# First head of a gated attention layer: four columns side by side from unnormalised x, the norm from x with tokens on partitions, and four plain gate columns

## The chip, the core and the metric

The kernel runs on one core of one Trainium2 chip. The metric is the device time of one execution in microseconds (us). The core's engines have queues of their own: TensorE (PE, with its weight loads PEld), VectorE (DVE), ScalarE (ACT), GpSimd (POOL) and SyncE (SP), which here issues nearly all transfers. They wait for each other by semaphores.

## What is computed

One layer with 512 tokens and a model width of 2048, all in float32, cut to what matters here:

```python
hn = rmsnorm(x, norm_g)                       # x: 512 tokens x 2048
proj = hn @ w_in                              # 3 branches x (q, k, v, gate) x 4 heads x 128 columns,
                                              # 4 forget logits, 3 x 2048 merge gate logits
...
yc = stick_breaking_attention(q, k, v)        # branch C, the first whose heads are computed here
ys = stack(ya, yb, yc) * silu(gate)
up = einsum('bsnw,nwd->bsnd', ys, w_up)
merged = sum(sigmoid(gates + b_gate) * up)
return x + merged @ w_out
```

`rmsnorm` divides each token by the root of the mean square over its 2048 values and multiplies by a gain for each of the 2048. A product of x with a weight column can therefore be made with the gain alone, and be multiplied by the token's factor afterwards.

## The kernel before

All activations lie transposed: 128 model values on the partitions, 512 tokens along the free side, sixteen such tiles of x (`xraw`, from `xT`). To keep float32's accuracy every operand is split into a high part (a copy on ACT, rounded to the product's format) and a low part (a subtraction on DVE), `split_to`, lines 91 to 93; a product of two operands is then three (`mm3`, lines 100 to 103).

The work of PE is a list of `units`. A unit has one weight tile of 8 k tiles x 128 columns (512 KB), loaded on SP, split on ACT and DVE (`prep`, two units ahead, `LA = 2`), and 24 products. There are two forms. A **plain column** (`col_task`) takes two units, one for each half of the 2048 rows, with 24 products of 512 tokens each. A **pair** (`pair_task`) computes two columns by Strassen's form in Winograd's variant: seven units with 24 products of 256 tokens each, in place of the four units of two plain columns. For that form the weight quarters are added on DVE (lines 315 to 327), the seven results are added up on DVE, and x is needed in other shapes: with x1 = [B11 | B12] and x2 = [B21 | B22] (halves of the model width by halves of the tokens) the parts B11, B21, B22, T1 = B12 - B11, T2 = B22 - T1, T3 = B22 - B12 and T4 = T2 - B21.

The first head (branch C, head 0) is made of plain columns, since it starts before the norm is known: `prep_x` (lines 217 to 230) splits x times its gain into `xs` and squares x on ACT; DVE and POOL add the squares up. Its ten units are: half of the forget logits (`f_units`, 16 products of 8 columns), q and k's first halves, the other half of the logits, q and k's second halves, then v and the gate. `norm_x` (line 244) sums the squares over the partitions by a product with ones, takes the root (`rsqrt`), and leaves the token factors `rstd`; it stands behind unit 1 with high priority. The column results are multiplied by `rstd` as they leave PSUM (`scaled`, line 626). From unit 3 on `combos(k)` multiplies x by gain and norm (line 255, DVE), forms T1 to T4's sums on POOL (lines 257 to 260) and splits them; `parts1` and `parts2` behind units 7 and 9 split the normalised x1 and x2, over the unnormalised ones. Two pairs of gate columns follow, and all further heads (q and k's pair, a gate pair, v and gate's pair, a gate pair). The stages of each head's attention are hung onto later units by `at(unit, work)`.

Tile's scheduler orders each engine's instructions by a simulation, except where a `manual_schedule` region keeps some engines in the order written: before, PE up to unit 17 (`OFF["man"]`, line 853). Pools: 21 tiles of 128x512 (`t2`), 56 for split x (`xt`), six raw weight tiles, three of each split weight, four PSUM tiles `acc` and four `att`.

Of the kernel before, what the change touches and what calls it, by code (L numbers as in the profile page):

```python
# [15 lines left out]
P = 128  # L16
S = 512
# [8 lines left out]
UK = 8  # L26
HS = S // 2
# [11 lines left out]
def hybrid_kernel(  # L39
    ctx: ExitStack,  # L40
    tc: tile.TileContext,
    xT: bass.AP,
    consts: bass.AP,
# [61 lines left out]
    # ------------------------------------------------------------------ constants  # L105
# [18 lines left out]
    class Unit:  # L124
        """A stretch of the tensor engine's work with one stationary operand of up to 8 k tiles."""
# [8 lines left out]
    def load(u):  # L134
        u.raw = []
        for s, keep in u.srcs:
            t = raw_tile(u.shape)
            nc.sync.dma_start(t, s)
            u.raw.append(t)
            if keep is not None:  # L140
                keep.append(t)
# [10 lines left out]

    for kt in range(4):
        load_x(kt)
# [18 lines left out]
    # -1 where key k >= j: suffix sums inside a block  # L173
# [4 lines left out]
    # A, rows are queries: NEG where the key (free) is after the query  # L178
# [4 lines left out]
    # C, rows are keys: valid where the query (free) is after the key  # L183
# [7 lines left out]
    # column h has ones on the rows h, 32 + h, 64 + h, 96 + h  # L191
# [6 lines left out]
    # the query gains carry the softmax scale  # L198
# [9 lines left out]
    t4 = [xt("t4") for _ in range(UK)]  # L208
    x1 = [(xt("x1h"), xt("x1l")) for _ in range(UK)]
    t23 = [(xt("t23h"), xt("t23l")) for _ in range(UK)]  # L210
    x2 = [(xt("x2h"), xt("x2l")) for _ in range(UK)]
    xs = x1 + x2
    ssq = [None, None]
    first_ps = att()
    sqp = [att(), att()]

    def prep_x(kt):
        x = xraw[kt]
        h, lo = xs[kt]
        if kt % 2:  # L220
            nc.vector.tensor_scalar_mul(h, x, gn[:, kt:kt + 1])
        else:
            nc.scalar.activation(h, x, AF.Copy, scale=gn[:, kt:kt + 1])
        nc.vector.scalar_tensor_tensor(lo, x, gn[:, kt:kt + 1], f(h), op0=ALU.mult, op1=ALU.subtract)
        s = sqp[kt // 2 % 2] if kt % 2 and kt > 1 else t2("sq")
        nc.scalar.activation(s, x, AF.Square)
        if kt < 2:
            ssq[kt] = s
        else:
            (nc.gpsimd, nc.vector)[kt % 2].tensor_add(ssq[kt % 2], ssq[kt % 2], s)  # L230

    def rsqrt(y, ps, n):
        """y = (ps / n + EPS) ** -0.5: a guess by exp and ln, and one Newton step."""
        t, w, v = t2("rt"), t2("rw"), t2("rv")
# [4 lines left out]
        nc.vector.tensor_mul(w, w, v)  # L239
        nc.vector.scalar_tensor_tensor(y, w, 1.5, t, op0=ALU.add, op1=ALU.mult)  # L240

    rstd = []

    def norm_x():
        ps = att()
        for i in range(2):
            nc.tensor.matmul(ps, onef, ssq[i], start=i == 0, stop=i == 1)
        rstd.append(t2("rstd"))
        rsqrt(rstd[0], ps, D)

    def combos(k):
        """The rows of x at their norm, and what Strassen's form needs of them beside the parts."""
        a, b = xraw[k], xraw[k + UK]
        for x, kt in ((a, k), (b, k + UK)):
            nc.vector.scalar_tensor_tensor(x, x, gn[:, kt:kt + 1], rstd[0], op0=ALU.mult, op1=ALU.mult)  # L255
        t, u = t2("t23"), t2("t4")
        nc.gpsimd.tensor_sub(t[:, RH], b[:, RH], a[:, RH])
        nc.gpsimd.tensor_sub(a[:, RH], a[:, RH], a[:, LH])
        nc.gpsimd.tensor_sub(t[:, LH], b[:, RH], a[:, RH])
        nc.gpsimd.tensor_sub(u[:, LH], t[:, LH], b[:, LH])  # L260
# [10 lines left out]
    # ------------------------------------------------------------------ projections  # L271
# [12 lines left out]
    def col_task(srcs, xs, evac):  # L284
        """A column tile as it stands; two units, one for each half of the rows."""
# [92 lines left out]
    # ------------------------------------------------------------------ attention  # L378
# [9 lines left out]
    def f_units():  # L388
        """The four heads' logits: the columns' high and low parts side by side."""
        w2 = cp.tile([P, KT, 2 * NH], F32R, name="w2")  # L390
        nc.vector.tensor_copy(w2[:, :, :NH], wf)
        nc.vector.tensor_sub(w2[:, :, NH:], wf, f(w2[:, :, :NH]))
        ps = first_ps

        def mms(i):
            def go(u):
                for kt in range(i * UK, (i + 1) * UK):
                    for j in range(2):
                        nc.tensor.matmul(ps[:2 * NH, :], w2[:, kt, :], xs[kt][j],
                                         start=kt + j == 0, stop=kt + j == KT)  # L400
            return go
        return [Unit(None, None, mms(i)) for i in range(2)], ps
# [4 lines left out]
    def forget_bias():  # L407
        """log sigmoid of the logits, their running sums, and the two sides of c[q] - c[k]."""
# [8 lines left out]
        # log1p(u) = 2 atanh(u / (2 + u))  # L417
# [29 lines left out]
    def tri(name, dt=F32):  # L447
        """Four tiles of 512, 384, 256 and 128 columns in three slots."""
        t = [t2(name, dt) for _ in range(3)]
        return [t[0], t[1][:, :S - P], t[2][:, :S - 2 * P], t[1][:, S - P:]]  # L450

    def head_stages(n, h, st):
        """The stages of a head's attention, as (units after the end of q and k, work)."""
# [110 lines left out]
        def av():  # L564
# [8 lines left out]
            # sigmoid(g) = exp(min(g, 0) - log(1 + exp(-|g|)))  # L573
# [26 lines left out]
    # ------------------------------------------------------------------ the order of the work  # L600
# [22 lines left out]
    def scaled(st, r):  # L623
        def evac(ps):
            st[r] = t2("c")
            nc.vector.tensor_mul(st[r], ps, rstd[0])
        return evac

    def first_head(n, h):
        st = {}  # L630
        fu, fps = f_units()
        c = {r: col_task(col(n, r, h), xs, scaled(st, r)) for r in (Q, K, V, G)}
        units.extend([fu[0], c[Q][0], c[K][0], fu[1], c[Q][1], c[K][1],
                      c[V][0], c[G][0], c[V][1], c[G][1]])

        def norm_first():
            with tc.high_priority():
                norm_x()
        at(1, norm_first)
        for k in range(UK):  # L640
            at(OFF["c0"] + k // OFF["c1"], lambda k=k: combos(k))

        def parts1():
            for k in range(UK):
                split_to(*x1[k], xraw[k])

        def parts2():
            for k in range(UK):
                split_to(*x2[k], xraw[k + UK])
            v = t2("f")[:2 * NH, :]  # L650
            nc.vector.tensor_mul(v, fps[:2 * NH, :], rstd[0][:2 * NH, :])
            nc.sync.dma_start(fd, v)
            at(12, forget_bias)
        at(7, parts1)
        at(9, parts2)
        a, b = head_stages(n, h, st)
        gate_units(late=OFF["l1"])
        gate_units(late=OFF["l2"])
# [5 lines left out]
    def head(n, h, last=False):  # L664
# [9 lines left out]
        if not last:  # L674
            gate_units()
# [17 lines left out]
    # merge gates and up projections  # L693
# [95 lines left out]
    # output projection  # L789
# [29 lines left out]
    # ------------------------------------------------------------------ emission  # L819
# [14 lines left out]
    prep_to(1)  # L834
    load_to(2)
    for kt in range(4, 8):
        load_x(kt)
    load_to(3)
    for kt in range(8, KT):
        load_x(kt)  # L840
    for kt in range(UK):
        prep_x(kt)
    prep_to(2)
    for kt in range(UK, KT):
        prep_x(kt)
        if kt == 11:
            prep_to(3)

    # the first head's products keep their order
    order = ExitStack()  # L850
    order.enter_context(tc.manual_schedule(engines={mybir.EngineType.PE}))
    for i, u in enumerate(units):
        if i == OFF["man"]:
            order.close()
        cur[0] = i
# [55 lines left out]
```

## Time and profile before

| | |
|---|---|
| time, median of 3 runs | 1399.99 us (1399.92 to 1400.05) |
| span of the profiled execution (first to last instruction) | 1397.6 us |
| around the span, to the median | 2.4 us |
| busy: PE, DVE, ACT, POOL | 1366.3, 1191.8, 729.7, 53.7 us |
| moved by DMA | 176.39 MB |

The page gives the profiled execution's span and no other time of its own. Busy times are sums over an engine's instructions. PE's rows overlap: the next product begins before the last has left the array, so a product's price is read from the distance between two starts, and not from its duration. In lists by line, `L93` and `L92` are the two lines of `split_to`, whoever calls it; the tile's name says which.

### The profile page before, as it was taken

The numbers are of one execution on the slowest core, as the hardware profiler recorded it, in microseconds if no ns is written. First come the engines' busy times: TensorE is split into PE (matmuls) and PEld (weight loads), VectorE is DVE, ScalarE is ACT, GpSimd is POOL, SyncE is SP. The second block draws the span as 40 slices with busy tenths as digits, with TensorE's granted clock in tenths as the row PEclk, the third lists the DMA queues.
The fourth block names the chain that finished last, engine by engine and source line by source line (L and its number), as shares of the span: only waits on it lengthen the run. The fifth ranks groups of instructions, "written<-read, shape, count | busy, mean of one in ns | idle before, by whom it ended". The sixth has DMA issues, their size and how long they took to land.

```text
span 1397.6 us, 25474 instructions
## 1 busy us (share of the span) xinstructions
PE 1366.3 (98%) x10452; PEld 1316.7 (94%) x10452; DVE 1191.8 (85%) x1671; ACT 729.7 (52%) x1042; POOL 53.7 (4%) x60
## 2 busy tenths in 40 slices
PE   6969999999999999999999999999999999999999
PEld 3759999999999999999999999999999988899999
DVE  8999898887978889888888888888888888898886
ACT  6345564544545555555556555545555755453332
POOL 4730000000000000000000000000000000000000
PEclk9989999999999999999999999999999999999999
DMA  7113334323344244342433333333233766535542
GB/s 272 46 46 106 122 102 126 121 91 114 106 129 126 95 114 128 113 129 95 117 122 115 121 94 119 113 114 121 91 115 103 273 197 203 169 109 176 164 151 76
DMA packets 63093, 176.39 MB, mean 126 GB/s; under 512 B 7400, under 2 KB 9320, under 8 KB 62976
## 3 DMA queue, kind: packets, MB, share of 16 engines
q1 hardware_dynamic: 59520, 170.49, 38.4%
q10 hardware_dynamic: 3456, 4.26, 0.8%
q8 instruction: 82, 1.34, 0.4%
q14 instruction: 35, 0.29, 0.1%
HBM read 155.04 MB, written 19.69 MB: 125 GB/s over the span
## 4 chain that ended last, share of the span: by engine, by line
PE 92%; DVE 5%; issue 1%; ACT 0%; POOL 0%; DMA 0%; SPq 0%; DVEq 0%; ACTq 0%; POOLq 0%
PE acc L101 27%; PE acc L103 27%; PE acc L102 27%; PE att L103 3%; PE att L101 3%; PE att L102 3%; DVE x L255 1%; DVE wl L93 1%; PE att L548 1%; PE att L517 1%; PE att L570 1%; DVE x1l L93 1%; PE att L571 1%; PE att L569 1%; DVE t23l L93 0%
## 5 line engine op out<-in xcount | busy, mean ns | idle before, releaser
L92 ACT ACTIVATE wh<-raw 128x1024 fp32r<-128x1024 f32 (+1 forms) x418 | 435.7, 1043 | 549.2 <-PE acc L102 488.2
L93 DVE TENSOR_TENSOR wl<-raw,wh 128x1024 fp32r<-128x1024 f32 (+1 forms) x418 | 503.9, 1206 | 96.7 <-ACT wh L92 95.9
L102 PE MATMUL acc<-x1l,wh 128*128 128x256 f32 (+1 forms) x768 | 222.3, 289 | 10.5 <-DVE x1l L93 10.5
L103 PE MATMUL acc<-x1h,wl 128*128 128x256 f32 (+1 forms) x768 | 222.0, 289 | 2.2 <-DVE wl L93 2.2
L101 PE MATMUL acc<-x1h,wh 128*128 128x256 f32 (+1 forms) x768 | 223.7, 291 | 0.0
L101 PE MATMUL acc<-x2h,wh 128*128 128x256 f32 (+1 forms) x768 | 223.6, 291 | 0.0
L102 PE MATMUL acc<-x2l,wh 128*128 128x256 f32 (+1 forms) x768 | 221.9, 289 | 0.9 <-DVE x2l L93 0.9
L103 PE MATMUL acc<-x2h,wl 128*128 128x256 f32 (+1 forms) x768 | 221.8, 289 | 0.0
L101 PE MATMUL acc<-t23h,wh 128*128 128x256 f32 x736 | 209.7, 285 | 0.0
L103 PE MATMUL acc<-t23h,wl 128*128 128x256 f32 x736 | 208.4, 284 | 0.0
L102 PE MATMUL acc<-t23l,wh 128*128 128x256 f32 x736 | 208.1, 283 | 0.0
L102 PEld LDWEIGHTS acc<-x1l,wh 128*128 128x128 f32 x768 | 147.8, 192 | 13.4 <-DVE x1l L93 11.2
L103 PEld LDWEIGHTS acc<-x1h,wl 128*128 128x128 f32 x768 | 147.8, 193 | 3.9 <-DVE wl L93 2.4
L102 PEld LDWEIGHTS acc<-x2l,wh 128*128 128x128 f32 x768 | 148.0, 193 | 2.4 <-DVE x2l L93 1.1
L101 PEld LDWEIGHTS acc<-x1h,wh 128*128 128x128 f32 x768 | 147.9, 193 | 1.8 <-issue 0.2
L101 PEld LDWEIGHTS acc<-x2h,wh 128*128 128x128 f32 x768 | 148.2, 193 | 1.3
L103 PEld LDWEIGHTS acc<-x2h,wl 128*128 128x128 f32 x768 | 148.0, 193 | 1.3
L101 PEld LDWEIGHTS acc<-t23h,wh 128*128 128x128 f32 x736 | 141.0, 192 | 0.5
L102 PEld LDWEIGHTS acc<-t23l,wh 128*128 128x128 f32 x736 | 141.0, 192 | 0.1
L103 PEld LDWEIGHTS acc<-t23h,wl 128*128 128x128 f32 x736 | 140.7, 191 | 0.3
L101 PE MATMUL acc<-t,wh 128*128 128x256 f32 x368 | 105.1, 286 | 0.0
L102 PE MATMUL acc<-t,wh 128*128 128x256 f32 x368 | 104.4, 284 | 0.0
(256 smaller groups left out, 2728.0 us busy)
## 6 DMA issues: line engine op xcount, KB each, us to landing
raw<-in_w_col SPq DMA_DIRECT2D x192, 512.0 KB, 3.6
raw<-in_w_out SPq DMA_DIRECT2D x32, 512.0 KB, 3.8
gl<-c SPq DMA_DIRECT2D x48, 256.0 KB, 2.0
raw<-in_w_up SPq DMA_DIRECT2D x32, 384.0 KB, 3.2
sg<-gl SPq DMA_DIRECT2D x48, 256.0 KB, 5.0
x<-in_xT SPq DMA_DIRECT2D x16, 256.0 KB, 5.4
xr<-in_xT SPq DMA_DIRECT2D x16, 256.0 KB, 4.4
yd<-y SPq DMA_DIRECT2D x11, 256.0 KB, 2.0
```

The costliest lines, as they stand in the source:

```text
L92: nc.scalar.activation(hi, src, AF.Copy)
L93: nc.vector.tensor_sub(lo, src, f(hi))
L101: nc.tensor.matmul(ps, lh, rh, start=start, stop=False)
L102: nc.tensor.matmul(ps, lh, rl, start=False, stop=False)
L103: nc.tensor.matmul(ps, ll, rh, start=False, stop=stop)
L255: nc.vector.scalar_tensor_tensor(x, x, gn[:, kt:kt + 1], rstd[0], op0=ALU.mult, op1=ALU.mult)
L517: nc.tensor.transpose(ps[:, blk(i)], st["p"][i][:, blk(j)], identf)
L548: nc.tensor.matmul(ps[:, i * P:], nu_r if i == j else nones_r, part, start=i == j and part is st["lk"][j][0], stop=False)
L569: nc.tensor.matmul(o, vh[:, blk(j)], st["h"][j], start=j == 0, stop=False)
L570: nc.tensor.matmul(o, vl[:, blk(j)], st["h"][j], start=False, stop=False)
L571: nc.tensor.matmul(o, vh[:, blk(j)], st["l"][j], start=False, stop=j == QB - 1)
```

## The change

The first head's q, k, v and gate are computed side by side, k tile after k tile, in eight units of two k tiles with four columns each (`first_quad`); the logits' products stand between. A weight tile of such a unit is gathered from four columns. x is first multiplied by its gain in place (`prep_x`: DVE up to tile 9, ACT from tile 10), then split. The norm comes from a second copy of x, `xn`, loaded with the tokens on the partitions in 16 pieces: ACT squares with a sum along the free side, DVE adds up, `rsqrt` works on a 128x4 tile, four diagonal blocks are made of it on ACT, and one product with ones spreads them over the partitions (`norm_rows`, behind k tile 6). `split_n` then multiplies x by the norm in place and splits it again over the old parts. `combos` works in place and on DVE alone, with half tiles; `split_t1` puts T1 over x1's right half. The first two gate pairs become four plain columns, whose first halves stand together and whose second halves follow; the third gate pair follows as a pair with T2 to T4 last, and the second head has one gate pair less. ACT and DVE keep the written order up to unit 16, PE up to unit 23. The number of columns is the same.

```diff
+NQ = 4
+    xn: bass.AP,
...
+            to = t
+            if len(s.shape) > len(t.shape):
+                to = t.rearrange("p (c k) m -> p c k m", c=s.shape[1])
+            nc.sync.dma_start(to, s)
...
     def prep_x(kt):
-        h, lo = xs[kt]
-        if kt % 2:
-            nc.vector.tensor_scalar_mul(h, x, gn[:, kt:kt + 1])
+        if kt < OFF["xg"]:
+            nc.vector.tensor_scalar_mul(x, x, gn[:, kt:kt + 1])
         else:
-            nc.scalar.activation(h, x, AF.Copy, scale=gn[:, kt:kt + 1])
-        nc.vector.scalar_tensor_tensor(lo, x, gn[:, kt:kt + 1], f(h), op0=ALU.mult, op1=ALU.subtract)
-        s = sqp[kt // 2 % 2] if kt % 2 and kt > 1 else t2("sq")
-        nc.scalar.activation(s, x, AF.Square)
-        if kt < 2:
-            ssq[kt] = s
-        else:
-            (nc.gpsimd, nc.vector)[kt % 2].tensor_add(ssq[kt % 2], ssq[kt % 2], s)
+            nc.scalar.activation(x, x, AF.Copy, scale=gn[:, kt:kt + 1])
+        split_to(*xs[kt], x)
+    def square_n(i):
+        nc.scalar.activation(xnat[i], xnat[i], AF.Square, accum_out=ssq[:, i // NQ, i % NQ:i % NQ + 1])
...
     def norm_x():
+        small_n = cp.tile([P, 5, QB], F32, name="small_n")
+        y, m, tmp = small_n[:, 0, :], small_n[:, 1, :], [small_n[:, i, :] for i in range(2, 5)]
+        nc.vector.tensor_reduce(m, ssq, axis=AX.X, op=ALU.add)
+        rsqrt(y, m, D, tmp)
+        dg = t2("dg")
+        for b in range(QB):
+            nc.scalar.activation(dg[:, blk(b)], identf, AF.Copy, scale=y[:, b:b + 1])
+        diag.append(dg)
+
+    def norm_rows():
         ps = att()
-        for i in range(2):
-            nc.tensor.matmul(ps, onef, ssq[i], start=i == 0, stop=i == 1)
+        nc.tensor.matmul(ps, onef, diag[0], start=True, stop=True)
         rstd.append(t2("rstd"))
-        rsqrt(rstd[0], ps, D)
+        nc.scalar.activation(rstd[0], ps, AF.Copy)
+
+    def split_n(kt):
+        nc.vector.tensor_mul(xraw[kt], xraw[kt], rstd[0])
+        split_to(*xs[kt], xraw[kt])
...
     def combos(k):
         a, b = xraw[k], xraw[k + UK]
-        for x, kt in ((a, k), (b, k + UK)):
-            nc.vector.scalar_tensor_tensor(x, x, gn[:, kt:kt + 1], rstd[0], op0=ALU.mult, op1=ALU.mult)
-        t, u = t2("t23"), t2("t4")
-        nc.gpsimd.tensor_sub(t[:, RH], b[:, RH], a[:, RH])
-        nc.gpsimd.tensor_sub(a[:, RH], a[:, RH], a[:, LH])
-        nc.gpsimd.tensor_sub(t[:, LH], b[:, RH], a[:, RH])
-        nc.gpsimd.tensor_sub(u[:, LH], t[:, LH], b[:, LH])
-        split_to(*t23[k], t)
-        split_to(t4[k][:, LH], t4[k][:, RH], u[:, LH])
+        t4.append(xt("t4"))
+        t23.append((xt("t23h"), xt("t23l")))
+        h, lo = t23[k]
+        nc.vector.tensor_sub(a[:, LH], a[:, RH], a[:, LH])
+        nc.vector.tensor_sub(a[:, RH], b[:, RH], a[:, RH])
+        nc.vector.tensor_sub(b[:, RH], b[:, RH], a[:, LH])
+        nc.vector.tensor_sub(b[:, LH], b[:, RH], b[:, LH])
+        split_to(h[:, LH], lo[:, LH], b[:, RH])
+        split_to(h[:, RH], lo[:, RH], a[:, RH])
+        split_to(t4[k][:, LH], t4[k][:, RH], b[:, LH])
+
+    def split_t1(k):
+        (h, lo), a = x1[k], xraw[k]
+        split_to(h[:, RH], lo[:, RH], a[:, LH])
...
+    def first_quad(st, n, h):
+        c0 = n * 4 * NH + h
+        ps = {r: Lazy(att if r in (V, G) else acc) for r in (Q, K, V, G)}
+        per = UK // 4
+
+        def mms(i):
+            def go(u):
+                for j in range(per):
+                    kt = i * per + j
+                    for r in (Q, K, V, G):
+                        c = r * per + j
+                        mm3(ps[r](), u.hi[:, c, :], u.lo[:, c, :], *xs[kt], kt == 0, kt == KT - 1)
+                    f_mms(kt)
+                    if kt == OFF["nrm"]:
+                        norm_rows()
+            return go
...
     def first_head(n, h):
-        units.extend([fu[0], c[Q][0], c[K][0], fu[1], c[Q][1], c[K][1],
-                      c[V][0], c[G][0], c[V][1], c[G][1]])
+        units.extend(first_quad(st, n, h))
+        nq = len(units)
+        cols = []
+        for _ in range(2):
+            g, d = gates.pop(0)
+            cols += [(g, d), (g, d + 1)]
+        t = [col_task(gate_col(*c), xs, spilled(*c)) for c in cols]
+        for i in range(2):
+            units.extend(u[i] for u in t)
+
+        def more_x(kt, n):
+            for k in range(kt, kt + 2):
+                prep_x(k)
+            for i in range(n, min(n + 4, NQ * QB)):
+                square_n(i)
+        at(0, lambda: more_x(6, 8))
+
+        def norm_first():
+            more_x(8, 12)
+            norm_x()
+        at(1, norm_first)
+        for i in range(2, 5):
+            at(i, lambda i=i: more_x(2 * i + 6, NQ * QB))
+        for kt in range(KT):
+            at(max(OFF["nrm"] // 2 + kt // 3, kt // 2), lambda kt=kt: split_n(kt))
+        for k in range(UK):
+            at(nq + k - 2 * (k < 1), lambda k=k: combos(k))
+            at(nq + 4 + k // 2, lambda k=k: split_t1(k))
+        at(OFF["fb"], forget_bias)
...
-        gate_units(late=OFF["l1"])
-        gate_units(late=OFF["l2"])
+        gate_units(late=True)
...
-        if not last:
+        if not last and (n, h) != (C, 1):
             gate_units()
...
+    load_x(0)
+    load_to(1)
+    for kt in range(1, 4):
+        load_x(kt)
+    load_to(2)
+    load_n4(0)
+    load_n4(1)
+    for kt in range(4, 6):
+        load_x(kt)
+    load_to(3)
...
+    begin = ExitStack()
+    begin.enter_context(tc.manual_schedule(engines={mybir.EngineType.Activation, mybir.EngineType.DVE}))
+    prep_x(0)
+    prep_to(1)
+    for kt in range(1, 4):
+        prep_x(kt)
+    prep_to(2)
+    for i in range(8):
+        square_n(i)
+    for kt in range(4, 6):
+        prep_x(kt)
...
+        if i == OFF["bgn"]:
+            begin.close()
...
-OFF = dict(cs=4, ct=12, nk=5, nq=4, s=12, t=16, v=1, av=8, a0=11, b0=18, c0=3, c1=2, man=17, last=3, l1=0, l2=0)
+OFF = dict(cs=4, ct=12, nk=5, nq=4, s=12, t=16, v=1, av=8, nrm=6, xg=10, bgn=16, fb=30, a0=16, b0=23, man=23, last=3)
```

The rest of `load_n4` and the loads alternates the pieces of `xn`, the tiles of x and the units' weights in the same way; `spilled` copies a plain gate column out of PSUM on ACT and stores it one unit later, as pairs do.

More of the change, by code (lines that the diff above doesn't have):

```diff
@@ L137, in load @@
             t = raw_tile(u.shape)
-            nc.sync.dma_start(t, s)
+            to = t
+            if len(s.shape) > len(t.shape):
+                to = t.rearrange("p (c k) m -> p c k m", c=s.shape[1])
+            nc.sync.dma_start(to, s)
             u.raw.append(t)
@@ L151, in prep_raw @@
         split_to(u.hi, u.lo, u.raw[0])
-    for kt in range(4):
-        load_x(kt)
     epsc = cp.tile([P, 1], F32, name="epsc")
@@ L386, in hybrid_kernel, with f_mms @@
     ylast = {}
[L388 to L402, printed above, removed]
+    w2 = cp.tile([P, KT, 2 * NH], F32R, name="w2")
+    nc.vector.tensor_copy(w2[:, :, :NH], wf)
+    nc.vector.tensor_sub(w2[:, :, NH:], wf, f(w2[:, :, :NH]))
+    def f_mms(kt):
+        for j in range(2):
+            nc.tensor.matmul(first_ps[:2 * NH, :], w2[:, kt, :], xs[kt][j], start=kt + j == 0, stop=kt + j == KT)
     bias = {}
@@ L893 @@
         "xT": g["x"][0].T.reshape(DT, P, S),
+        "xn": g["x"][0].reshape(QB, P, DT // NQ, S).transpose(0, 2, 1, 3),
         "consts": np.concatenate(consts, axis=1),
```

78 lines of the change are left out of this document (42 added, 36 removed).

## The prediction

> **What bounds the kernel now.** First the busy times by stretch, to see where TensorE (PE) is not full. Columns: stretch, its length, then busy us (instructions) of each engine, granted clock, DMA share, GB/s.
>
> ```profile
> 0.00:20.20 20.20, 7.78 (x16) 1.19 (x17) 16.09 (x28) 12.40 (x19) 11.20 (x23) 1.00 0.94 350
> 20.20:72.07 51.87, 51.87 (x214) 40.09 (x214) 49.57 (x59) 22.45 (x35) 29.93 (x25) 1.00 0.24 78
> 72.07:95.36 23.29, 9.67 (x49) 8.56 (x48) 23.29 (x28) 11.44 (x20) 11.05 (x10) 0.71 0.01 1
> 95.36:140.00 44.64, 44.64 (x370) 44.42 (x369) 41.33 (x76) 23.88 (x37) 0.00 (x0) 1.00 0.40 121
> ```
>
> From 95 us on PE is full (44.64 of 44.64); the change can earn only what the first 95 us lose. Second, PE in order of time there: start, us, instruction, wait.
>
> ```profile
> 4.91 0.59 PE L399 MATMUL att<-x1h,w 128*8 128x512 f32 x1 [4.91 <-DVE identb L172]
> 20.16 0.59 PE L399 MATMUL att<-x1l,w 128*8 128x512 f32 x1 [3.28 <-DVE x1l L224]
> 20.55 0.63 PE L101 MATMUL acc<-x1h,wh 128*128 128x512 f32 x1
> 25.64 0.40 PE L101 MATMUL acc<-x1h,wh 128*128 128x512 f32 x1
> 28.14 0.39 PE L103 MATMUL acc<-x1h,wl 128*128 128x512 f32 x1
> 28.37 2.00 PE L247 MATMUL att<-sq,tmpc 128*128 128x512 f32 x4
> 29.81 0.79 PE L101 MATMUL acc<-x1h,wh 128*128 128x512 f32 x1
> ...
> 72.07 0.28 PE L101 MATMUL acc<-x1h,wh 128*128 128x256 f32 x1
> 72.18 0.28 PE L102 MATMUL acc<-x1l,wh 128*128 128x256 f32 x1
> 74.65 0.39 PE L103 MATMUL acc<-x1h,wl 128*128 128x256 f32 x1 [2.19 <-DVE wl L93]
> 74.87 0.28 PE L101 MATMUL acc<-x1h,wh 128*128 128x256 f32 x1
> 74.99 0.28 PE L102 MATMUL acc<-x1l,wh 128*128 128x256 f32 x1
> 81.47 0.58 PE L102 MATMUL acc<-x1l,wh 128*128 128x256 f32 x1 [4.18 <-DVE x1l L93]
> 88.75 0.58 PE L102 MATMUL acc<-x1l,wh 128*128 128x256 f32 x1 [6.27 <-DVE x1l L93]
> 95.36 0.28 PE L101 MATMUL acc<-t23h,wh 128*128 128x256 f32 x1
> ```
>
> Prices by start-to-start: at the full clock a product of 512 columns takes 0.227 us (11 from 25.64 to 28.14), of 256 columns 0.120 (74.87 to 74.99); at the half clock 0.425 (12 from 20.55 to 25.64). The clock rose 5.1 us after steady work began at 20.55, and was half again after the idle 4.18 us, but not after the idle 2.19 us.
>
> The ledger to the end of the first head and three pairs (six gate or q and k columns), which both kernels compute first. At full speed: 32 logit and 192 column products x 0.227 = 50.8; norm 1.4 (28.37 to 29.81); a pair is 7 x 24 x 0.120 = 20.2, three 60.5; sum 112.7. In fact: at 95.36 two of the first pair's seven products are done; the other five take 14.4, to 109.8, and two pairs more end at 150.1 (attention's own products left out on both sides). **Lost: 37.4 us**: some 17 before 20.55, 2.4 to the half clock behind it, some 17.5 in the first pair.
>
> What PE waits for there is VectorE (DVE), busy 23.29 of 23.29 us, with GpSimd (POOL) running beside it and slowing it:
>
> ```profile
> L93 DVE TENSOR_TENSOR x1l<-x,x1h 128x512 fp32r<-128x512 f32 x8 | 8.9, 1153 | 0.0
> L255 DVE SCALAR_TENSOR_TENSOR x<-x,small_in,rstd 128x512 f32<-128x512 f32 x16 | 14.6, 983 | 0.0
> L93 DVE TENSOR_TENSOR qkl<-c,qkh 128x512 fp32r<-128x512 f32 x8 | 5.5, 682 | 0.0
> L260 POOL TENSOR_TENSOR t<-t,x 128x256 f32<-128x256 f32 x8 | 9.3, 1160 | 0.6
> ```
>
> The same subtraction costs 1153 ns while POOL works and 682 without it.
>
> **The change, part by part.** DVE and ACT prices, start to start, and the handover between them:
>
> ```profile
> 92.82 0.41 DVE L93 TENSOR_TENSOR t<-t,t 128x256 fp32r<-128x256 f32 x1
> 93.16 1.21 DVE L93 TENSOR_TENSOR wl<-raw,wh 128x1024 fp32r<-128x1024 f32 x1
> 94.30 0.67 DVE L93 TENSOR_TENSOR x2l<-x,x2h 128x512 fp32r<-128x512 f32 x1
> 94.90 1.20 DVE L93 TENSOR_TENSOR wl<-raw,wh 128x1024 fp32r<-128x1024 f32 x1
> ...
> 10.96 0.48 DVE L221 TENSOR_SCALAR x1h<-x,small_in 128x512 fp32r<-128x512 f32 x1
> 11.35 0.68 DVE L230 TENSOR_TENSOR sq<-sq,att 128x512 f32<-128x512 f32 x1
> ...
> 6.31 0.23 DVE L190 CAST mskc<-tmpc 128x128 bf16<-128x128 f32 x1
> ```
>
> ```profile
> 95.44 1.06 ACT L92 ACTIVATE wh<-raw 128x1024 fp32r<-128x1024 f32 x1 [4.69 <-PE acc L102]
> 96.41 0.61 ACT L92 ACTIVATE qkh<-c 128x512 fp32r<-128x512 f32 x1
> 96.93 0.20 ACT L416 ACTIVATE lf<-lf 128x16 f32<-128x16 f32 x1
> ...
> 57.23 0.63 ACT L92 ACTIVATE t23h<-t 128x512 fp32r<-128x512 f32 x1 [5.88 <-POOL t L259]
> 57.89 0.69 DVE L93 TENSOR_TENSOR t23l<-t,t23h 128x512 fp32r<-128x512 f32 x1 [2.12 <-ACT t23h L92]
> ```
>
> DVE: 0.34 (256 columns), 0.60 (512), 1.14 (1024), 0.39 (scaling). ACT: 0.97 (1024), 0.52 (512). A result crosses 0.03 us after its row ends (57.23 + 0.63, 57.89), so a consumer elsewhere starts some 0.11 after the next instruction at home could.
>
> *Products.* Two pairs become plain columns: 96 x 0.227 = 21.8 for 20.2 each, **+3.2 us**. The norm's two fp32 products become one, about -0.4 with the clock then half. The logits' 32 products stay, spread over the first eight units (28 products, 6.35 us each). At full speed the ledger is 115.5.
>
> *Start.* First heavy product at 20.55 before. Now: DVE is through its constants between 4.9 (the row at 4.91 waits for one of them) and 6.5 (6.31 + 0.23), 5.6 taken; then scale x0 0.40, copy 0.53, weight copy 0.97, handovers: **7.7**. Then some 2.8 at half clock.
>
> *Order.* ACT and DVE issue the region up to unit 16 as written, as PE does its own now (the norm at 28.37 stands behind Q's 24th product). Each split is then a chain: DVE multiplies, ACT copies, DVE subtracts, and the next multiply stands behind that subtraction. A scaled x tile: 0.40 + 0.11 + 0.53 + 0.11 + 0.60 = 1.75; a normalised one 0.60 in place of 0.40, 1.95; a weight tile 1.14, plus some 0.4 in which DVE waits for its copy.
>
> *To the norm.* ACT: x0 to x3 and two weights to 14.3, eight squares to 19.4, x4, x5, weight 2 to 22.6, x6, x7, four squares, weight 3 to 30.1, x8, x9, four squares to 36.7, the small chain and four diagonal blocks to 39.7. No row shows a square with sums; the nearest is this, 0.51 + 0.09 for 384 columns:
>
> ```profile
> 468.06 0.61 ACT L506 ACTIVATE p<-p,mx 128x384 f32<-128x384 f32 x1
> 468.57 0.19 ACT L506 ACTIVATION_READ_ACCUMULATOR p<-p,mx 128x1 f32 x1
> 468.66 0.59 ACT L92 ACTIVATE vh<-att 128x512 fp32r<-128x512 f32 x1
> ```
>
> 0.63 for 512 columns is taken; 0.52 (no cost for the sum) to 0.81 (its whole row), at sixteen squares, moves this by -1.8 to +2.9, and the end by as much. PE reaches the norm's product at 34.2 and waits **5.7**, with everything behind it; small waits before that sum to 2.1. The clock falls.
>
> *The long chain.* From 47.9 DVE has: 15 normalised tiles 29.3, two late x tiles 1.2 to 2.0, five weights 7.7, five evacuations 3.0, one set of combinations 2.6: to 92.4. PE, past the norm and its unit at 46.7, has units 4 to 9 in that time, 4 x 6.35 + 2 x 5.44 = 36.3 us, which would end at 83. So two plain columns' weights come late (their halves are split in the chain at 81 to 82 and 91 to 92): waits of **3.8 and 3.1** at units 9 and 10, and a third fall of the clock between them, without which the second wait would be that much longer. Without POOL, DVE's prices hold.
>
> *T1.* Combinations for k 1 to 7 take some 2.5 to 3 us each beside 5.44 of PE: hidden. T1's splits and the pair's weight sums end at 135; the third product of the pair (unit 18) waits **3.9** in two units.
>
> *Moved.* The first head's attention starts five units later and the forget bias eighteen, with the instructions they had; both lie under PE's full stretch (from 95.36 on DVE has 41.33 of 44.64 us busy and still keeps PE full), and DVE sheds two pairs' weight sums and recombinations there. The four gate columns are stored by the same four transfers. If that cover were gone, the 41.33 would have to grow by over 3 us in 45 to show.
>
> *Transfers.* Four MB more of x, ahead of weights 2 to 5. At 350 GB/s the 11.5 MB up to weight 5 land by 36, while ACT takes that weight at 43: hidden by the chain. Weights now come in runs of 1 KB; no row shows a load of that kind. At half the rate for their 3 MB they land 9 us later, still only 2 late; at the full rate 0.
>
> *Sum.* 115.5 + start 7.7 + waits 18.5 (2.1, 5.7, 3.8, 3.1, 3.9) + three half-clock spells of 5.1 us each, of which 2.3 on the mean is lost, 7.0 = **148.7 against 150.1: -1.4 us**. Behind that both have the same products, and the tail is untouched. Span 1397.6 - 1.4 = 1396.2; the median lies 2.4 above the span: **1398.6 us**.
>
> The clock rows above (2.19 kept, 4.18 lost) leave open which wait of mine between them costs it. The Trainium skill (TensorE: Matmul & The Clock Gate, section What's actually happening) sets the idle window at about 3.4 us, free-running; by that rule waits of 3.5 may go either way, and the sum stands between 148.7 and, if a wait of 2.3 cools too, 152.8.
>
> **Rivals.**
> *Slower: DVE pays whole rows.* If the 0.08 us by which DVE's instructions overlap is lost in this alternation (0.68, 1.22, 0.41 as in the rows' second column), the long chain grows and units 8 to 10 and 17, 18 wait longer: my queue ends at 153.9, **1403.8 us**. For it: dependent DVE instructions do not overlap, the multiply of the norm's root starts 0.79 behind its predecessor:
>
> ```profile
> 33.82 0.68 DVE L239 TENSOR_TENSOR rw<-rw,rv 128x512 f32<-128x512 f32 x1
> 34.61 0.69 DVE L240 SCALAR_TENSOR_TENSOR rstd<-rw,rt 128x512 f32<-128x512 f32 x1
> ```
>
> Against: the subtractions and the next tile's multiply do not depend on each other. It decides from 0.62 us a multiply on, where gain turns to loss.
> *Faster: the chain is not serial.* If the multiply of the next tile runs under the copy of the last, a tile costs 1.2 to 1.3, the waits at units 9 and 10 vanish, the queue ends at 139.6: **1389.5 us**. Against: DVE stood 2.12 us idle at 57.89 with work behind it. The Trainium skill (TensorE: Matmul & The Clock Gate, section Architectural detail) says ScalarE and VectorE take their queues strictly in order; by that rule only another written order gives this time, and that row agrees.
> *It does not do what it says:* the plain columns bring no cover because the combinations still end last. That is the T1 wait, 3.9 above.
>
> **How the numbers follow.** Forecast 0.55, its own range 1394 to 1403 (squares -1.8 to +2.9, start -0.6 to +0.7, clock up to +4.1); slower rival 0.25; faster rival 0.20. No change means within 0.2%, 2.8 us. The forecast splits 0.4, 0.5, 0.1: faster 0.20 + 0.22 = 0.42, same 0.28 + 0.02 = 0.30, slower 0.28. Range 1388 to 1406: both rivals, the slower with the clock's share.
>
> **What would show it.** First L101-kind product near 7.7 us; the norm's product with a wait of 4 to 7 near 40; DVE alternating with idle of about 0.75 us per tile from 48 to 92; PE waiting for weights in units 9 and 10, and for T1 or weights in the third product of the pair near 133; first pair's end near 149. Wrong if DVE shows no such idle, if the quad's products stay at 0.425, or if x or weights land after they are wanted.

## The result, and the profile after

| | before | after |
|---|---|---|
| time, median | 1400.02 us (1399.92 to 1400.70, 4 runs) | 1408.26 us (1407.18 to 1409.21, 4 runs) |
| span of the profiled execution | 1397.6 us | 1406.6 us |
| busy: PE, DVE, ACT, POOL | 1366.3, 1191.8, 729.7, 53.7 us | 1372.6, 1167.0, 738.1, 4.3 us |

The ratio is 1.0054 (95% interval 1.0040 to 1.0069): slower by 8.2 us, where 1.4 us faster was forecast, and above the range. From 178 us on PE is full again; nearly all that differs lies ahead of that. One of the four runs of e10 below took 2685.26 us, and without it that run's median of 1387.74 is 1387.55.

The windows of the changed kernel, as in the first view of before (length, busy us of PE, PEld, DVE, ACT, POOL, granted clock, DMA share, GB/s):

```profile
20.00:50.00 30.00, 24.23 (x92) 16.52 (x92) 14.90 (x23) 20.85 (x47) 0.00 (x0) 0.89 0.81 281
50.00:75.00 25.00, 24.92 (x109) 18.61 (x107) 16.93 (x24) 11.37 (x17) 0.00 (x0) 1.00 0.16 45
75.00:110.00 35.00, 27.07 (x99) 20.47 (x98) 29.55 (x67) 12.64 (x24) 0.00 (x0) 0.85 0.25 80
...
135.00:160.00 25.00, 21.75 (x165) 21.21 (x164) 21.92 (x35) 11.45 (x20) 0.00 (x0) 0.93 0.34 100
```

PE is short in three of these four stretches, and each of the three has a clock below 1. No engine is full there: DVE has 29.55 of 35 us, where before it had all of the 23.29. An engine that waits and is waited for, and is full nowhere, is a chain.

PE's main waits in that kernel in order of time, with products at the half clock behind them:

```profile
8.95 0.79 PE L103 MATMUL acc<-x1h,wh 128*128 128x512 f32 x1 [8.95 <-ACT wh L94]
...
13.79 0.63 PE L104 MATMUL att<-x1l,wh 128*128 128x512 f32 x1
...
41.00 2.04 PE L260 MATMUL att<-dg,tmpc 128*128 128x512 f32 x2 [5.24 <-ACT dg L255]
...
44.55 0.63 PE L104 MATMUL acc<-x1l,wh 128*128 128x512 f32 x1
...
82.83 0.80 PE L103 MATMUL acc<-x1h,wh 128*128 128x512 f32 x1 [4.02 <-ACT wh L94]
...
85.54 0.63 PE L105 MATMUL acc<-x1h,wl 128*128 128x512 f32 x1
85.96 0.44 PE L103 MATMUL acc<-x1h,wh 128*128 128x512 f32 x1
...
94.11 0.80 PE L103 MATMUL acc<-x1h,wh 128*128 128x512 f32 x1 [3.83 <-ACT wh L94]
...
99.38 0.56 PE L105 MATMUL acc<-x1h,wl 128*128 128x512 f32 x1
99.78 0.39 PE L103 MATMUL acc<-x1h,wh 128*128 128x512 f32 x1
...
132.91 0.39 PE L103 MATMUL acc<-x2h,wh 128*128 128x256 f32 x1 [0.17 <-ACT wh L94]
...
142.80 0.38 PE L103 MATMUL acc<-x1h,wh 128*128 128x256 f32 x1 [3.04 <-ACT x1h L94]
...
144.09 0.41 PE L103 MATMUL acc<-x2h,wh 128*128 128x256 f32 x1
...
147.07 0.41 PE L105 MATMUL acc<-x2h,wl 128*128 128x256 f32 x1
...
157.94 0.28 PE L103 MATMUL acc<-x1h,wh 128*128 128x256 f32 x1
...
175.47 0.68 PE L564 MATMUL att<-lkh,nu_r 128*128 128x512 f32 x2 [1.87 <-ACT lkh L94]
```

The rows at 82.83 and 94.11 are the first products of units 9 and 10, the one at 142.80 is the third product of the pair (unit 18) at T1 of k tile 7, and the one at 157.94 begins the second pair. A duration of 0.63 for 512 columns is the half clock, 0.39 the full one; for 256 columns it is 0.41 and 0.28. Behind 94.11 the half clock lasts until some 99.6 us.

DVE in the long chain:

```profile
50.37 0.69 DVE L95 TENSOR_TENSOR x1l<-x,x1h 128x512 fp32r<-128x512 f32 x1 [0.70 <-ACT x1h L94]
50.98 0.69 DVE L266 TENSOR_TENSOR x<-x,rstd 128x512 f32<-128x512 f32 x1
52.36 0.69 DVE L95 TENSOR_TENSOR x1l<-x,x1h 128x512 fp32r<-128x512 f32 x1 [0.70 <-ACT x1h L94]
```

Subtraction to subtraction is 1.99 us a tile, and 0.70 of it DVE stands idle for ACT's copy.

### The profile page after: what moved, and what is told of

Read it like the earlier page. It is cut to its first block, busy times and chain, and to the rows that moved or that the text cites. A ratio compares the mean times of both kernels' runs of the same rounds, so it can differ in the third digit from the quotient of the medians.

```text
span 1406.6 us, 25159 instructions
## 1 busy us (share of the span) xinstructions
PE 1372.6 (98%) x10306; PEld 1314.1 (93%) x10306; DVE 1167.0 (83%) x1687; ACT 738.1 (52%) x1090; POOL 4.3 (0%) x21
## 4 chain that ended last, share of the span: by engine, by line
PE 92%; DVE 4%; ACT 3%; issue 1%; DMA 1%; SPq 0%; ACTq 0%; DVEq 0%
PE acc L103 26%; PE acc L105 26%; PE acc L104 26%; PE att L105 3%; PE att L103 3%; PE att L104 3%; DVE wl L95 1%; ACT wh L94 1%; PE att L564 1%; ACT xn L233 1%; PE att L533 1%; PE att L586 1%; PE att L587 1%; PE att L585 1%; DMA x<-in_xT 0%
## 5 line engine op out<-in xcount | busy, mean ns | idle before, releaser
L94 ACT ACTIVATE wh<-raw 128x1024 fp32r<-128x1024 f32 (+1 forms) x412 | 429.2, 1042 | 507.0 <-PE acc L104 447.1
L95 DVE TENSOR_TENSOR wl<-raw,wh 128x1024 fp32r<-128x1024 f32 (+1 forms) x412 | 495.3, 1202 | 100.8 <-ACT wh L94 99.8
L103 PE MATMUL acc<-t23h,wh 128*128 128x256 f32 x704 | 200.8, 285 | 0.0
L105 PE MATMUL acc<-t23h,wl 128*128 128x256 f32 x704 | 199.3, 284 | 0.0
L104 PE MATMUL acc<-t23l,wh 128*128 128x256 f32 x704 | 199.1, 283 | 0.0
L103 PEld LDWEIGHTS acc<-x2h,wh 128*128 128x128 f32 x752 | 144.6, 192 | 3.1 <-ACT wh L94 0.4
L103 PEld LDWEIGHTS acc<-t23h,wh 128*128 128x128 f32 x704 | 134.9, 192 | 0.3
L105 PEld LDWEIGHTS acc<-t23h,wl 128*128 128x128 f32 x704 | 134.6, 192 | 0.4
L104 PEld LDWEIGHTS acc<-t23l,wh 128*128 128x128 f32 x704 | 135.0, 192 | 0.0
L103 PE MATMUL acc<-t,wh 128*128 128x256 f32 x352 | 100.6, 286 | 0.0
L104 PE MATMUL acc<-t,wh 128*128 128x256 f32 x352 | 99.8, 284 | 0.0
```

Of the source, the lines that this page charges most:

```text
L94: nc.scalar.activation(hi, src, AF.Copy)
L95: nc.vector.tensor_sub(lo, src, f(hi))
L103: nc.tensor.matmul(ps, lh, rh, start=start, stop=False)
L104: nc.tensor.matmul(ps, lh, rl, start=False, stop=False)
L105: nc.tensor.matmul(ps, ll, rh, start=False, stop=stop)
```

## The experiments

Before took 1399.9 to 1400.6 us beside them. Units count from 0; the runs are called e1 to e12, as in their labels.

**Forget bias, and a longer ordered region.** The forget bias stood at unit 30 in the text, but the scheduler put its small instructions into DVE's ordered part. In the changed kernel:

```profile
88.92 0.68 DVE L266 TENSOR_TENSOR x<-x,rstd 128x512 f32<-128x512 f32 x1
90.75 0.23 DVE L430 SCALAR_TENSOR_TENSOR lf<-lf,small_in 128x16 f32<-128x16 f32 x1 [1.15 <-DMA lf<-fd]
91.01 0.17 DVE L431 SCALAR_TENSOR_TENSOR lf<-lf 128x16 f32<-128x16 f32 x1
91.11 0.68 DVE L95 TENSOR_TENSOR x2l<-x,x2h 128x512 fp32r<-128x512 f32 x1
...
94.09 1.23 DVE L95 TENSOR_TENSOR wl<-raw,wh 128x1024 fp32r<-128x1024 f32 x1
```

DVE waits 1.15 us for a transfer of `lf`, with the split that unit 10's weights stand behind queued after it. Other instructions from behind the region slipped in likewise, among the steps of the last combination. Three runs:

```diff
-OFF = dict(... bgn=16, fb=30, ...)
+OFF = dict(... bgn=16, fb=15, ...)    # e1_forget_last
+OFF = dict(... bgn=19, fb=30, ...)    # e2_order_to_19
+OFF = dict(... bgn=19, fb=15, ...)    # e3_both
```

> Forget bias written at the end of the ordered region (behind the last split of T1) instead of at unit 30. Theory (unordered small instructions on DVE between 90 and 100 us make unit 10's weights late, and waits over 3 us halve the clock): the wait of 3.83 us at unit 10 shrinks to 2 us or less, no clock fall behind it, first pair's third unit starts 3 to 5 us earlier, time 1403.5 to 1406. Rival 1 (the 3.2 us of plain products and the norm's 5.2 us wait are all of the loss): nothing moves, 1408 +- 1. Rival 2 (DVE's whole work up to T1 decides, wherever it stands): unit 10 is earlier but T1's wait grows by as much, 1408 +- 1.

> Written order of ACT and DVE kept up to unit 19 instead of 16, so that the weights of units 18 to 20 and the attention's first splits cannot stand between the last combinations. Theory: the third unit of the first pair loses its 3.04 us wait for T1 or most of it, and no half clock follows: 1403.5 to 1406. Rival 1 (products and norm wait): 1408 +- 1. Rival 2 (DVE's whole work decides): T1 comes earlier but the weights of units 19 and 20 are as late as T1 was, 1407 to 1409.

> Both edits of the two runs before. Theory: the waits at unit 10 and at T1 shrink together, 1400 to 1403. Rival 1 (products and norm wait): 1408 +- 1. Rival 2 (DVE's whole work): 1406 to 1409, the wait goes to the weights behind T1.

Measured: 1406.94 (ratio 1.0048, 1.0033 to 1.0063), 1408.88 (1.0062, 1.0047 to 1.0077) and 1411.73 (1.0083, 1.0068 to 1.0098). Unit 10's wait in the first run and unit 18's in the second:

```profile
93.32 0.50 PE L103 MATMUL acc<-x1h,wh 128*128 128x512 f32 x1 [1.95 <-ACT wh L94]
```

```profile
139.48 0.39 PE L103 MATMUL acc<-x1h,wh 128*128 128x256 f32 x1 [2.26 <-ACT wh L94]
...
140.74 0.41 PE L105 MATMUL acc<-x1h,wl 128*128 128x256 f32 x1 [0.75 <-DVE wl L95]
```

The wait at unit 10 falls from 3.83 to 1.95 as expected, but the run gains 1.3 us, not 2 to 5: less than the theory. The runs of the two kernels touch (1407.18 to 1409.21 and 1406.59 to 1407.22); in the traces unit 17 starts 1.2 us earlier (131.70 for 132.91). With the longer region T1 is in time and unit 18's weights are late in its place; nothing is won, and both edits together lose 3.5 us. My theory on the unordered instructions at T1 fell: what was put between was wanted as soon itself, and rival 2 held (the third run is slower still than it said).

**The order of the chain.** Same instructions, DVE's next multiply ahead of its subtraction:

```diff
 def split_n(kt):
-    nc.vector.tensor_mul(xraw[kt], xraw[kt], rstd[0])
-    split_to(*xs[kt], xraw[kt])
+    if kt == 0:
+        nc.vector.tensor_mul(xraw[0], xraw[0], rstd[0])
+    hi, lo = xs[kt]
+    nc.scalar.activation(hi, xraw[kt], AF.Copy)
+    if kt + 1 < KT:
+        nc.vector.tensor_mul(xraw[kt + 1], xraw[kt + 1], rstd[0])
+    nc.vector.tensor_sub(lo, xraw[kt], f(hi))
```

> Normalised split in another written order: DVE's multiply of tile k+1 stands before its subtraction for tile k, so that it runs while ACT copies; same instructions. Theory (a serial chain of DVE, ACT, DVE of 1.95 us a tile is what makes the plain columns' weights late): a tile takes 1.25 to 1.35, the waits of 4.02 and 3.83 us at units 9 and 10 vanish with their two clock falls, time 1397 to 1401. Rival 1 (products and norm wait): 1408 +- 1. Rival 2 (DVE is bound by its busy time, not by the chain): the tiles take 1.7 or more, 1406 or more.

Measured: **1394.89** (0.9963, 0.9949 to 0.9977), 13.4 us less than the changed kernel, faster than before, and a larger gain than the 1397 to 1401 expected. DVE of this run, and its windows:

```profile
50.43 0.69 DVE L272 TENSOR_TENSOR x1l<-x,x1h 128x512 fp32r<-128x512 f32 x1
51.04 0.69 DVE L271 TENSOR_TENSOR x<-x,rstd 128x512 f32<-128x512 f32 x1
51.64 0.69 DVE L272 TENSOR_TENSOR x1l<-x,x1h 128x512 fp32r<-128x512 f32 x1
```

```profile
50.00:75.00 25.00, 25.00 (x111) 19.05 (x110) 23.72 (x39) 14.84 (x24) 0.00 (x0) 1.00 0.20 64
75.00:110.00 35.00, 35.00 (x156) 29.00 (x155) 29.95 (x73) 15.93 (x32) 0.00 (x0) 1.00 0.36 107
```

A tile takes 1.21 us, the idle of 0.70 is gone, DVE is at work for 23.72 of 25 us and PE is full from 50 to 110: the waits of 4.02 and 3.83 are gone with the half clock behind both. The waits at the norm (5.24) and at T1 (3.03) stay. The order as written, and no instruction's price, was what cost.

**The norm's wait.** Its product behind k tile 7 (`nrm=6` to `nrm=7`), alone:

> The norm's product stands behind k tile 7's products instead of k tile 6's, so that PE does 14 products more before it waits. Theory (DVE's chain of splits, not PE, sets when units 9 and 10 can start): the norm's wait falls from 5.24 to some 2 us and unit 4 starts 4 to 5 us earlier, but the chain starts when it did, unit 9's wait grows by as much, and the time stays: 1407.5 to 1409. Rival 1 (the norm's wait and the half clock behind it are the loss): 1403 to 1405.

Measured: 1408.06 (1.0059, 1.0042 to 1.0076). The norm's wait falls to 2.02, unit 4 starts at 41.97 in place of 47.11, and unit 9 still at 82.93 (82.83 in the changed kernel). Five us won on PE are lost again in front of DVE's chain.

**The clock.** Products of constants ahead of the late units:

```diff
+DUMMY = {9: 10, 10: 17, 18: 8}
...
+    def keep_busy(n):
+        if n:
+            ps = att()
+        for _ in range(n):
+            nc.tensor.matmul(ps[:, :P], identf, identf, start=True, stop=True)
...
+        keep_busy(DUMMY.get(i, 0))
         u.mms(u)
```

> PE is kept at work in three waits: 10, 17 and 8 products of two constant tiles (128 columns, fp32, results not read) stand ahead of units 9, 10 and 18, some 2.5, 4.2 and 2 us, so that what is left of each wait is under 2.2 us. Nothing else moves. Theory (each wait over 3 us halves the clock behind it, and behind units 10 and 18 nothing takes that loss up): unit 9 to 11 and 18 run at the full clock, 2 to 2.5 us won behind unit 10 and as much behind T1, time 1403 to 1405. Rival (the clock has no part in it, the waits alone do): 1408 +- 1.

Measured: 1404.82 (1.0036, 1.0023 to 1.0049), 3.4 us less. PE of this run at unit 10:

```profile
89.15 3.96 PE L896 MATMUL att<-identf 128*128 128x128 f32 x34
94.00 0.50 PE L103 MATMUL acc<-x1h,wh 128*128 128x512 f32 x1 [0.89 <-ACT wh L94]
```

Unit 10 starts when it did (94.00 for 94.11), so DVE's and ACT's work is unmoved up to there; it ends at 100.38 in place of 102.51, and the granted clock in 75 to 110 us is 1.00 in place of 0.85. From T1's wait to unit 20 it takes 3.81 us in place of 5.29. So the half clock behind the waits at units 10 and 18 costs 3.4 us by itself; what is lost behind unit 9 is taken up by the wait at unit 10.

**T1, and the norm's wait again.** On the kernel with the next multiply first; there DVE stood idle 3.13 us ahead of T1's first splits:

```profile
96.47 1.23 DVE L95 TENSOR_TENSOR wl<-raw,wh 128x1024 fp32r<-128x1024 f32 x1 [0.47 <-ACT wh L94]
100.83 0.76 DVE L95 TENSOR_TENSOR x1l<-x,x1h 128x256 fp32r<-128x256 f32 x2 [3.13 <-ACT x1h L94]
```

```diff
-            at(nq + k - 2 * (k < 1), lambda k=k: combos(k))
+            at(nq + k - 2 * (k < 1) - (k > 3), lambda k=k: combos(k))
```

> The kernel with the next tile's multiply first, and in it the combinations of k 4 to 7 one unit earlier each. Theory (T1 is late because DVE stands idle for 3.13 us at 97.7 us, behind ACT's evacuation of the first plain column, with the combinations written behind it): that idle is filled, T1's wait of 3.03 us goes and the half clock with it, 1389 to 1392. Rival (what stands between the last combinations unordered, two splits of q and k and the pair's weights, makes T1 late): 1394 to 1396.

> The run before with the norm's product behind k tile 7 as well. Theory: once the chain no longer sets units 9 and 10, PE's norm wait does, so the edit that gives nothing by itself gives 2 to 4 us here: 1386 to 1389. Rival (DVE's whole work up to T1 sets the end): as the run before, within 1 us.

Measured: 1391.30 (0.9938, 0.9924 to 0.9953) and, with `nrm=7` added, 1391.85 (0.9937, 0.9922 to 0.9952). T1's wait is gone; it was the order of the combinations, by an idle that the order made. The norm's edit gives nothing here either, as its rival said, but the rival's cause (DVE's whole work) is not shown by the traces. Unit 10 now waits 1.0 us, and unit 17 1.7 in place of 0.9. PE is still 1.7 us ahead behind unit 17's second wait (120.05 for 121.76), and then runs at the half clock twice, from 120.5 and from 158.3 us, where the run without the edit does not in its trace (rows in the last section). One of the four runs took 1389.04.

**One plain pair in place of two.**

```diff
-        for _ in range(2):
+        for _ in range(1):
             g, d = gates.pop(0)
...
-            at(nq + k - 2 * (k < 1), lambda k=k: combos(k))
-            at(nq + 4 + k // 2, lambda k=k: split_t1(k))
+            at(nq + (k - 1) // 2 - (k < 1), lambda k=k: combos(k))
+            at(nq + 2 + k // 4, lambda k=k: split_t1(k))
...
-        if not last and (n, h) != (C, 1):
+        if not last:
```

(The unit numbers of the regions and of the first head's attention are four smaller.)

> The changed kernel with two plain gate columns in place of four; the other pair goes by seven products again, as before, and the combinations are written two to a unit. Rival 1 (the plain products' 3.2 us are pure loss): their half comes back, 1406 to 1407. Theory (they are cover for DVE's work on the combinations): T1 is due 10.9 us earlier, DVE has two columns' weights (4.6 us) and some 5 of the 10 us in which it stood idle between 75 and 135 less to go through, so T1's wait grows by 1 to 4 us and eats the 1.6: 1408 to 1412.

Measured: 1418.95 (1.0133, 1.0118 to 1.0149), 10.7 us more than with two, outside of both expectations:

```profile
123.31 0.58 PE L103 MATMUL acc<-x2h,wh 128*128 128x256 f32 x1 [8.19 <-ACT wh L94]
```

The first Strassen pair meets its weights 8.19 us late, since they stand behind the combinations in the written order (ACT copies them at 122.22, right behind the combinations' copies). That is how this run, with two combinations to a unit, wrote them; another order was not tried. I had let DVE's idle time take up half of the cover that goes, but most of that idle lies inside a chain, as I read it, and takes nothing up. In this order the plain columns' 3.2 us of products are cheap for what they cover.

**The first head's sums.** In the changed kernel's attention, the last split came late (row at 175.47). The scores one unit earlier, on the kernel with combinations early; and that with `nrm=7` and `fb=15` too:

```diff
-            g += [(OFF["cs"] + i, stick_scores(QB - 1 - i)) for i in range(QB)]
+            g += [(OFF["cs"] - (h == 0) + i, stick_scores(QB - 1 - i)) for i in range(QB)]
```

> The kernel with the next tile's multiply first and the combinations early, and in it the first head's score products and their splits one unit earlier. Theory (the wait of 1.87 us at the first head's sums comes from DVE taking its splits last, behind two pair sums and two weight splits): the wait shrinks to under 0.5, 1389 to 1390.5. Rival (the same DVE work is only moved, another wait takes its place): 1391 to 1392.5.

> The run before with the norm's product behind k tile 7 and the forget bias written at the end of the ordered region. Theory (with the norm's wait short, DVE's work between 70 and 93 us sets unit 10; 2.9 us of small forget bias instructions leave it): unit 10's wait of about 1 us goes, T1 comes earlier, 1386 to 1388.5. Rival (DVE's whole work to unit 20 sets the end, wherever the forget bias stands): 1390 to 1392.

Measured: 1387.74 (0.9908, 0.9888 to 0.9928) and **1387.50** (0.9907, 0.9893 to 0.9922). The wait of 1.87 is gone from the list of waits in both. The first gained 3.6 us over the kernel it was made from and came out below the expected 1389 to 1390.5; the wait explains 1.9. Between the profiled runs of the two it is 2.7, and the other 0.9 is there already at unit 17 (120.88 for 121.76), ahead of the edit. The medians of the two new kernels do not differ. The second came out in its expected range only because the first was faster than expected; unit 10's wait, which was to go, is still 1.15. Its profiled run (1386.34) has a granted clock of 1.00 and is 1.6 us below the first one's, and its other three (1387.42 to 1387.70) have 0.998: that the clock took the gain there fits this, but no profile of those runs shows it. Either kernel is some 13 us faster than before.

**Three terms at once, the splits left serial.** The changed kernel with `fb=15`, the scores one unit earlier and 10, 14 and 8 products of constants:

> The changed kernel with the three things mended that the forecast left out or mis-sized, its splits in their serial order: forget bias written at the end of the ordered region, PE kept at work in the waits ahead of units 9, 10 and 18 (10, 14 and 8 products), the first head's scores one unit earlier. Theory (three separate terms: 1.3 for the forget bias, 3.5 for two clock falls, 1.9 for the wait at the first head's sums): they add to 6.7, 1401.6, within 1 us. Rival (they share one cause, DVE's whole work, and what one gives the other takes): 1403.5 to 1405.

Measured: 1403.31 (1.0019, 1.0010 to 1.0029), 5.0 us less than the changed kernel where 6.7 were expected, between the theory (within 1 us of 1401.6) and the rival (1403.5 to 1405). Four of its eleven runs took 1401.71 to 1402.10, the other seven 1403.22 to 1404.02. The profiled one (1403.41) has the half clock behind a wait of 1.45 us at T1, here with the next products:

```profile
140.03 0.39 PE L103 MATMUL acc<-x1h,wh 128*128 128x256 f32 x1 [1.45 <-ACT x1h L94]
...
141.04 0.42 PE L103 MATMUL acc<-x2h,wh 128*128 128x256 f32 x1
```

The run that kept the clock (e6) has a wait of 1.44 at the same place and keeps it:

```profile
140.66 0.38 PE L103 MATMUL acc<-x1h,wh 128*128 128x256 f32 x1 [1.44 <-ACT x1h L94]
...
141.59 0.28 PE L103 MATMUL acc<-x2h,wh 128*128 128x256 f32 x1
```

From unit 19's start to unit 20's it is 4.57 us in the one and 2.88 in the other; 0.28 of the difference is a score product that stands there now, and 1.4 the clock. That is the distance of the two groups of runs too. If the four faster ones are those that kept the clock, the three terms add as expected there. No profile shows it; the granted clocks on record, 0.996 to 0.997 for the four and 0.995 to 0.996 for the seven, lean that way.

## Why the prediction was wrong

**What held.** The mechanism: the ordered region makes a serial chain of the splits. Forecast and measured: a normalised tile 1.95 and 1.99; the norm's product near 40 with a wait of 5.7, and 41.00 with 5.24; waits at units 9 and 10 of 3.8 and 3.1, and 4.02 and 3.83; T1's third product with 3.9 in two units, and 3.04 beside 0.17, 0.76 and 0.21. Each of these is within 1.1 us. A kernel without the chain has the forecast gain and more: the rival "the chain is not serial" priced another written order at 1389.5, and e4, which is that edit alone, took 1394.89. The 1391.30 and 1387.74 of e7 and e10, around the rival's price, needed further edits.

**What failed: the term for the clock.** The sum had "three half-clock spells of 5.1 us each, of which 2.3 on the mean is lost, 7.0". There were five: at the start, behind the norm, and behind each of the waits at 82.83, 94.11 and 142.80. I had let unit 9's and unit 10's waits share one and given T1's none, though in the prediction's nearest row an idle 4.18 us was followed by the half clock. Keeping PE at work in these three waits gave back 3.4 us (e6): alone enough to turn a gain of 1.4 into a loss. The spells lasted from 3.1 us (behind 82.83) to some 5.4 (behind 94.11), where 5.1 was priced. The whole sum says the same. The first pair ends at 157.94 us, 156.7 without the 1.2 us of score products in it, where 148.7 was forecast: 8.0 late. The waits came to 17.8 in place of 18.5 and the start to 1.25 more. The five spells lost some 11.3 in place of 7.0, an estimate from the starts of their products (2.86, 1.85, 1.82, 2.95 and 1.85, with 0.227 or 0.120 taken off for each product; pauses too short to be listed as waits are in it).

**What failed: "Behind that both have the same products, and the tail is untouched."** The first head's attention has the instructions that it had, but not the same company: at its sums PE waits 1.87 us, which before it did not. The forecast asked whether DVE has room there, and not which of its instructions comes last.

**What failed: the forget bias "under PE's full stretch".** Its place in the text was unit 30; where it stood is decided by the scheduler, which slipped it between the ordered instructions at 90 us. Undoing it gave 1.3 us (e1).

**A smaller size.** The start came at 8.95 in place of 7.7: x tile 0 was there at 6.80 us, where DVE had been taken as the last to be ready, at 5.6.

```profile
6.80 0.49 DVE L220 TENSOR_SCALAR x<-x,small_in 128x512 f32<-128x512 f32 x1 [1.80 <-DMA x<-in_xT]
```

Taken one by one the four are 3.4 + 1.9 + 1.3 + 1.25 = 7.9 of the 9.7 us between 1398.6 and 1408.3. The first and the third were undone alone. The 1.9 is the length of the wait, which was undone only on another kernel (e10) and together with others (e12); the start's was only read from the row, and no run undid it. The first three undone at once gave 5.0 (e12), or 6.4 in its four faster runs, so that with the start's 1.25 some 2.0 to 3.5 us of the 9.7 stay open. Eight first units of 6.44 us (starts 47.11 and 53.55, say) in place of 6.35 would make up 0.7 of them.

**The other terms.** The slower rival, whole rows on DVE, did not happen in the chain: DVE's instructions follow each other by 0.60 to 0.61 (50.37 and 50.98). In the combinations' half-tile steps it did (last section). Squares with sums were 0.61 apart where 0.63 was taken. Behind x tile 0 the transfers of x and of the weights were hidden by the chain, as forecast; the plain products' 3.2 stand, and e9 shows, for its order, that they buy more than they cost.

## What to carry to other kernels

A written order across two engines turns work that could overlap into a chain wherever a tile goes forth and back between them: write the next tile's first step ahead of this tile's last step, and compare DVE's busy time with its span before looking for shorter instructions. When a forecast has several waits on a clocked engine, count a loss of the clock behind each one, and do not let two waits share it. An instruction without a fixed order beside ones with an order may land among them, so a move in the text is no move on the chip until the engine's order has been read.

## What the runs showed of the hardware

The clock falls after much shorter waits than I had priced, and not each time. After 1.44 us it stayed (e6), after 1.45 it fell (e12), and in the run with `nrm=7` and early combinations (e8) two short waits were enough:

```profile
118.79 0.39 PE L103 MATMUL acc<-x2h,wh 128*128 128x256 f32 x1 [0.91 <-ACT wh L94]
120.05 0.39 PE L105 MATMUL acc<-x2h,wl 128*128 128x256 f32 x1 [0.76 <-DVE wl L95]
...
120.39 0.27 PE L104 MATMUL acc<-x2l,wh 128*128 128x256 f32 x1
120.50 0.34 PE L105 MATMUL acc<-x2h,wl 128*128 128x256 f32 x1
120.64 0.42 PE L103 MATMUL acc<-x2h,wh 128*128 128x256 f32 x1
...
123.85 0.35 PE L103 MATMUL acc<-x2h,wh 128*128 128x256 f32 x1
124.04 0.28 PE L104 MATMUL acc<-x2l,wh 128*128 128x256 f32 x1
```

Here the half clock begins some 0.5 us after PE is back at work, between two products, and lasts 3.3 us (120.5 to 123.85). A wait of 1.87 us at the first head's sums kept it in the changed kernel, and 2.19 us kept it before; in e8 the wait of 1.87 lost it (0.28 for 256 columns at the full clock):

```profile
157.41 0.68 PE L569 MATMUL att<-lkh,nu_r 128*128 128x512 f32 x2 [1.87 <-ACT lkh L94]
...
158.28 0.42 PE L569 MATMUL att<-lkl,nones_r 128*128 128x256 f32 x1
```

The Trainium skill (TensorE: Matmul & The Clock Gate, section What's actually happening) speaks of a free-running window of about 3.4 us: the length of the spell at 120.5 and its beginning at no edge of a wait agree with a window that runs by itself. That it takes a whole idle window does not agree: no wait from 42 us up to that spell was longer than 0.91. A share of idle time within a window could fit all these rows, but was not tested by itself.

DVE's half-tile steps on one tile stand 0.46 us apart, here in the run with the next multiply first:

```profile
101.50 0.42 DVE L280 TENSOR_TENSOR x<-x 128x256 f32<-128x256 f32 x1
101.96 0.43 DVE L281 TENSOR_TENSOR x<-x,x 128x256 f32<-128x256 f32 x1
102.42 0.42 DVE L282 TENSOR_TENSOR x<-x,x 128x256 f32<-128x256 f32 x1
```

The forecast took 0.34, from half tiles that share nothing: a step on the tile just written waits for the row before to end. With the forget bias's small instructions in between they are as far apart (98.77, 99.22 and 99.68 in the changed kernel), so those came nearly free there.
